# Low parts of the keys on all 128 rows: a second score product with 128 rows instead of 64

## The chip, the cores and the metric

The kernel runs on one core of one Trainium2 chip. The metric is the device time of one execution in microseconds. The kernel before has a median of 1945.59 us over 3 runs (1942.4 to 1946.55). Five engines work side by side, each on its own list of instructions, and wait for one another by semaphores: TensorE (PE, matrix products), VectorE (DVE), ScalarE (ACT), GpSimd (POOL) and SyncE (SP, which issues the transfers).

## The reference

Two layers over 512 latent tokens and 256 context tokens of width 1024: attention with a feed-forward part, then a gated linear recurrence with another. Only attention is touched:

```python
q_l = apply_axial_rope(rms_norm(q, q_norm), rope)      # 16 heads of 64
k_all = concat([rms_norm(k_ctx), apply_axial_rope(rms_norm(k_lat))])   # 4 key heads, 768 keys
s = einsum('bkgqd,bksd->bkgqs', q, k) * 64 ** -0.5     # float32
p = softmax(s); o = einsum('bkgqs,bksd->bkgqd', p, v)
y = o @ w_o
```

Four query heads share a key head. Latent queries see all 768 keys, context queries the 256 context keys.

## The kernel before, in words

The products run in a short float32 form (float32r). To keep float32 accuracy, an operand is split into a high part (rounded to the short form) and a low part (the rest), and the products high by high, high by low and low by high are added in one PSUM bank (`mm3`, L105 to L107, for the projections).

**Tiles.** Tokens come in 6 tiles of 128 (4 latent, 2 context). A head has 64 numbers per token, so after a transpose a head fills 64 rows. The 128 rows of a query tile hold both parts of the same head: the high part on one half and the low part on the other (`qd`, L545 and L546; which half is high depends on whether the key head g is even). The high keys stand twice, once on each half (`kd`, L525, written in both places before the transpose), so that one product of 128 rows gives high query by high key plus low query by high key (L606). The low keys of two key heads share one tile, one on each half (`kTl`), and the second product (L607) takes just the 64 rows with the high query: high query by low key.

**Preparation.** Queries and keys are made in `qk_norm_rope`, in units of two token tiles: 3 key units and 12 query units. A unit is squared on ACT (L479, tile `qsq`), reduced and turned into a scale on DVE and ACT (L482 to L489), scaled (L491, `qhat`), rotated on DVE and POOL (L501 to L510, tiles `qrot`, two buffers, and `qsin`), split into high and low (L525 and L526 for keys, L545 and L546 for queries), then transposed by PE into a PSUM bank and copied out by ACT (L537 for keys, L555 for queries). While a unit goes through this chain, PE makes the projections of the following ones (`q`, four PSUM banks). The transposes of a unit are issued three units later (`Q_LAG`).

**The attention loop.** 16 heads by 6 query tiles make 96 units. Each step of the loop issues the score products of unit i (two PSUM buffers `sc`; max on DVE L647, exponential on ACT L649, reciprocal on DVE L650, scaling on POOL L651), the transposes of unit i-3 (PE L661; ACT casts the high part `pth`, DVE subtracts the low part `ptl`), and every second step the product with the values of units up to i-6 (PE L672 and L673, collected in `ofp`). When two heads are complete, their outputs are split into `oh` and `ol` (three buffers each), and after four heads the output projection (`wo`) is run piece by piece between the units.

**What sets the order.** The code is written with these lags, and when the program is built a scheduler may let an instruction change places with others of its engine. The order is then fixed; each engine takes its list in that order.

Of the kernel before, what the change touches and what calls it, by code (L numbers as in the profile page):

```python
# [8 lines left out]
F32 = mybir.dt.float32  # L9
F32R = mybir.dt.float32r  # L10
# [6 lines left out]
P = 128  # L17
# [4 lines left out]
T = NL + NC  # L22
NT = T // P
NLT = NL // P
EPS = 1e-6
HEADS = 16
KVH = 4
HD = 64
# [15 lines left out]
def kernel(  # L44
# [10 lines left out]
    PE, DVE, ACT, POOL = nc.tensor, nc.vector, nc.scalar, nc.gpsimd  # L55
    dma = nc.sync.dma_start

    def pool(name, es=None, **kw):
        return (es or ctx).enter_context(tc.tile_pool(name=name, bufs=1, reuse_waits="tile", **kw))
# [76 lines left out]

    pes = psum_pool(s2=3, b=2)

# [1 line left out]
    ident = cst.tile([P, P], F32, name="ident")  # L140
    make_identity(nc, ident)
    ones = cst.tile([P, P], F32, name="ones")
# [84 lines left out]
        return ring.tile([P, 1024], F32, tag="raw", bufs=4, name=name)  # L227


# [1 line left out]
    def sumsq_add(acc, sqp, h, k, first, eng=None):  # L231
        if first:
            ACT.activation(acc, h, AF.Square)
        else:
            sq = sqp.tile([P, T], F32, tag="sq", bufs=2, name=f"sq{k}")
            sq = sq[:, : h.shape[1]]
            ACT.activation(sq, h, AF.Square)
            (eng or DVE).tensor_tensor(acc, acc, sq, op=ALU.add)
# [53 lines left out]
        lo = [pl.tile([P, T], F32R, name=f"hnl{k}") for k in range(KT)]  # L292
        return hi, lo

    # ================= layer 0: attention =================
    qes = ctx.enter_context(ExitStack())
    hnp = pool("hn0p", qes, side="right")
    hn_hi, hn_lo = hn_tiles(hnp)
    qst = pool("qkvst", qes, side="right")

# [1 line left out]
    vvs = ctx.enter_context(ExitStack())  # L302
    vvp = pool("vvp", vvs)
    vvt = vvp.tile([P, NT, KVH, P], F32R, name="vv")
# [36 lines left out]
    for t in range(NT):  # L341
        r = rs0[:, t : t + 1]
# [44 lines left out]
    for k in range(KT):  # L387
        ps = s2(f"ptx{k}")
        for t in range(NT):
            PE.transpose(ps[:, t * P : (t + 1) * P], xt[t][:, k * P : (k + 1) * P], ident)  # L390
        h = stp.tile([P, T], F32, name=f"xhT{k}")
# [3 lines left out]
            DVE.tensor_copy(h, ps[:, 0:T])  # L395
        xhT.append(h)

    kraw = qst.tile([P, NT, 256], F32, tag="kraw", name="kraw")
    accs = [s2(f"kv{i}") for i in range(3)]
    acc = [accs[t // 2][:, (t % 2) * 512 : (t % 2) * 512 + 512] for t in range(NT)]  # L400
    def kv_load(k0, n):
# [30 lines left out]
    DVE.tensor_copy(cols2[:, 16:48], pr[:, 0:32])  # L432
    st.close()

# [1 line left out]
    att = ctx.enter_context(ExitStack())  # L436
    keep = pool("attkeep", att)

    def qt_tile(g):
        return keep.tile([P, 4, T], F32R, tag=f"qT{g}", name=f"qT{g}")  # L440

    qT = [qt_tile(g) for g in range(KVH)]
    kTt = keep.tile([P, KVH + KVH // 2, T], F32R, name="kT")
    kTh = [kTt[:, g] for g in range(KVH)]
    kTl = [kTt[:, KVH + i] for i in range(KVH // 2)]

    ropec = qst.tile([P, NLT, HD], F32, name="ropec")
    ropes = qst.tile([P, NLT, HD], F32, name="ropes")
    dma(ropec, rope_cos.rearrange("(t p) d -> p t d", p=P))
    dma(ropes, rope_sin.rearrange("(t p) d -> p t d", p=P))  # L450
    tabs = {}
# [19 lines left out]
    def qk_norm_rope(src, tp, nm, eng=POOL):  # L471
        w, cw, sw = tabs[nm]

        def tmp(tag, bufs=1):
            tt = qst.tile([P, 512], F32, tag=tag, bufs=bufs, name=tag)
            return tt.rearrange("p (t h d) -> p t h d", t=2, d=HD)

        sq = tmp("qsq")
        ACT.activation(sq, src, AF.Square)  # L479
        sst = qst.tile([P, 3, 8], F32, tag="ss", bufs=2, name="ss")  # L480
        ss, sr, sa = sst[:, 0], sst[:, 1], sst[:, 2]
        DVE.tensor_reduce(ss, sq.rearrange("p t h d -> p (t h) d"), op=ALU.add, axis=AX.X)  # L482
        DVE.tensor_scalar(ss, ss, 1.0 / HD, EPS, op0=ALU.mult, op1=ALU.add)
        ACT.activation(sr, ss, AF.Sqrt)
        DVE.reciprocal(sr, sr)
        DVE.tensor_tensor(sa, sr, sr, op=ALU.mult)
        DVE.tensor_tensor(sa, sa, ss, op=ALU.mult)
        DVE.tensor_scalar(sa, sa, -0.5, 1.5, op0=ALU.mult, op1=ALU.add)
        DVE.tensor_tensor(ss, sr, sa, op=ALU.mult)  # L489
        qh = tmp("qhat")  # L490
        DVE.tensor_tensor(qh, src, ss.rearrange("p (t h) -> p t h", t=2).unsqueeze(3).to_broadcast([P, 2, 4, HD]),  # L491
                          op=ALU.mult)
        r = tmp("qrot", 2)
        if tp == 2:
            eng.tensor_tensor(r.rearrange("p t h d -> p (t h) d"), qh.rearrange("p t h d -> p (t h) d"),
                               w.unsqueeze(1).to_broadcast([P, 8, HD]), op=ALU.mult)
            return r
        sn = tmp("qsin")
        for tt in range(2):
            t = tp * 2 + tt  # L500
            DVE.tensor_tensor(r[:, tt], qh[:, tt], cw[:, t].unsqueeze(1).to_broadcast([P, 4, HD]), op=ALU.mult)  # L501
            sn5 = sn[:, tt].rearrange("p h (a b i) -> p h a b i", a=2, b=2)
            q5 = qh[:, tt].rearrange("p h (a b i) -> p h a b i", a=2, b=2)
            t5 = sw[:, t].rearrange("p (a b i) -> p a b i", a=2, b=2)
            for b in range(2):
                POOL.tensor_tensor(
                    sn5[:, :, :, b], q5[:, :, :, 1 - b],
                    t5[:, :, b].unsqueeze(1).to_broadcast([P, 4, 2, 16]), op=ALU.mult,
                )
        DVE.tensor_tensor(r, r, sn, op=ALU.add)  # L510
        return r

    for i in range(NT // 2):
        kv = accs[i].rearrange("p (t n) -> p t n", t=2)
        vsrc = kv[:, :, 256:512].rearrange("p t (g d) -> p t g d", d=HD)
        dst = vvt[:, 2 * i : 2 * i + 2]
        ACT.copy(kraw[:, 2 * i : 2 * i + 2], kv[:, :, 0:256])
        split(dst[:, :, :, 0:HD], dst[:, :, :, HD:P], vsrc)

    def k_first(tp):  # L520
        r = qk_norm_rope(kraw[:, 2 * tp : 2 * tp + 2].rearrange("p t (h d) -> p t h d", d=HD), tp, "k")
        kd = qst.tile([P, 2, KVH, 2, HD], F32R, tag="sp", bufs=3, name="kd")
        kl = qst.tile([P, 2, KVH, HD], F32R, tag="spl", name="kl")
        for i in range(2):
            DVE.tensor_copy(kd[:, :, :, i].rearrange("p t h d -> p (t h) d"), r.rearrange("p t h d -> p (t h) d"))  # L525
        POOL.tensor_tensor(kl, r, kd[:, :, :, 0].bitcast(F32), op=ALU.subtract)  # L526

        def second():
            kds = [kd[:, :, g].rearrange("p t a d -> p t (a d)") for g in range(KVH)]
            kds += [kl[:, :, 2 * i : 2 * i + 2].rearrange("p t a d -> p t (a d)") for i in range(KVH // 2)]  # L530
            for i in range(0, len(kds), 2):
                pt = bank("ptk")
                for j in range(2):
                    for tt in range(2):
                        PE.transpose(pt[:, (2 * j + tt) * P : (2 * j + tt + 1) * P],
                                     kds[i + j][:, tt].bitcast(F32), ident)
                ACT.copy(kTt[:, i : i + 2, tp * 256 : tp * 256 + 256], pt.rearrange("p (g t) -> p g t", g=2))  # L537

        return second

# [55 lines left out]

    def score_mm(h, t):
        g, j = h // 4, h % 4
        hrow = slice((g % 2) * HD, (g % 2) * HD + HD)
        keys = key_tiles(t)  # L600
        nk, k0 = len(keys) * P, keys[0] * P
        q = qT[g][:, j, t * P : (t + 1) * P]
        ps = s2("sc")
        for a in range(0, nk, 512):
            e = min(nk, a + 512)
            PE.matmul(ps[:, a:e], q, kTh[g][:, k0 + a : k0 + e], start=True, stop=False)  # L606
            PE.matmul(ps[:, a:e], q[hrow], kTl[g // 2][hrow, k0 + a : k0 + e], start=False, stop=True)  # L607
        return ps

    dfill.drain()  # L610
# [28 lines left out]
    ap_ = pool("att", att)  # L639
# [54 lines left out]
    fill.add(residual_in())  # L694
    pfill.add(ada_chunk(4, None, lambda: ap_.tile([P, T], F32, tag="pf", bufs=4, name="arows"), ring_raw))
    units = [(h, t) for h in range(HEADS) for t in range(NT)]
    pfs, pts, ofps, ohs = {}, {}, {}, {}

    def second(h, t):
        if t % 2 == 0:  # L700
# [6 lines left out]
    def third(h, t):  # L707
        if t % 2 == 0:
            return
        if h % 2 == 0 and t == 1:  # L710
            ofps[h // 2] = ap_.tile([P, T], F32, tag="sq", bufs=2, name="ofp")
        pv_prod(h, t // 2, *pts.pop((h, t // 2)), ofps[h // 2])
        if h % 2 == 1 and t == NT - 1:
            a = ap_.tile([P, T], F32R, tag="oh", bufs=3, name="oh")
            b = ap_.tile([P, T], F32R, tag="ol", bufs=3, name="ol")
            split(a, b, ofps.pop(h // 2), DVE if h == HEADS - 1 else POOL)
            ohs[h // 2] = (a, b)
            if h % 4 == 3:
                g = h // 4
                prs = [ohs.pop(2 * g), ohs.pop(2 * g + 1)]  # L720
                fill.add(wo_gen(g, [p_[0] for p_ in prs], [p_[1] for p_ in prs]))
# [15 lines left out]
    pes.close()  # L737
    pes = ctx.enter_context(psum_pool(s2=3, b=2))

    # ================= feed-forward =================  # L740
    def ffn(layer, only_lat, begin, late, pre=None, tail=None):
        n = NL if only_lat else T
        spans = SP2[:1] if only_lat else SP2
# [215 lines left out]

    ffn(0, False, lambda fill, fp: fill.add(ada_ffn(0, 5, fp)), ada_last, tail=norm_tail)  # L960

    # ================= layer 1: gated linear recurrence =================
    hg = ExitStack()
    hop = pool("hgrno")
    hp = pool("hgrn", hg)
# [312 lines left out]
```

## Time and profile before

| What | Value |
|---|---|
| Runs | 1945.59 us median, 1942.4 to 1946.55 |
| Span of the profiled execution | 1940.9 us, 4.7 us below the median; no other time is recorded for it |
| PE busy over the span | 1881.8 us, 97% |
| DVE, ACT, POOL busy | 1128.3 us (58%), 679.6 us (35%), 394.6 us (20%) |
| Score products, first and last start | 173.3 and 454.3 us |
| Preparation of queries and keys | to 173.3 us; the last 80 us of it are 95 to 175 us |
| Mean granted clock of PE | 0.992 |

Busy shares over the whole span mix stages with different limits, so the stretches are read apart. In the order of time, durations on PE overlap: a product's cost there is the distance between its start and the next start. A row of waits names the waiting engine and line, what it waited for, the total in us, how often, and the longest. "issue" means that an engine stood still without waiting for anything that the profile shows.

### The profile page before, as it was taken

What the parts mean: (1) busy time and instruction counts of PE and PEld (TensorE: products, weight loads), DVE (VectorE), ACT (ScalarE), POOL (GpSimd) and SP (SyncE); (2) the same over time, 40 slices, a digit from 0 to 9 for tenths busy, and PEclk for the clock granted to TensorE, in tenths of its full rate; (3) what the DMA queues carried; (4) which work ended last, traced back from release to release, by engine and by line L of the source; (5) the groups of instructions that cost most, each with busy time, mean ns of one, the idle gap of its engine ahead of it and who ended that gap; (6) DMA issues with size and microseconds to landing.
All of it is one profiled execution on the core that took longest, in us unless ns stands there. A gap on an engine that the chain in (4) does not pass through costs nothing. (4 is left out here: it accounts for less than half of the span.)

```text
span 1940.9 us, 29657 instructions
## 1 busy us (share of the span) xinstructions
PE 1881.8 (97%) x12111; PEld 1636.6 (84%) x12111; DVE 1128.3 (58%) x1815; ACT 679.6 (35%) x1219; POOL 394.6 (20%) x401
## 2 busy tenths in 40 slices
PE   8999999999999999999999999999999899999998
PEld 6787677777888888888887888989898799898997
DVE  4675677776993736544545546464656754344444
ACT  3334766564422112212222523333233332222224
POOL 1253434332200000000001434453446100000000
PEclk9999999999999999999999999999999999999999
DMA  9434100001442425433422111211211133333321
GB/s 327 160 99 141 55 1 23 4 20 46 128 147 60 152 60 153 138 98 118 139 68 75 51 55 38 66 55 55 65 34 44 44 99 96 90 95 90 98 81 61
DMA packets 206152, 166.37 MB, mean 86 GB/s; under 512 B 6801, under 2 KB 189249, under 8 KB 206017
## 3 DMA queue, kind: packets, MB, share of 16 engines
q1 hardware_dynamic: 205728, 163.43, 27.3%
q8 instruction: 96, 1.57, 0.3%
q10 hardware_dynamic: 288, 1.05, 0.1%
q14 instruction: 40, 0.32, 0.1%
HBM read 162.36 MB, written 2.10 MB: 85 GB/s over the span
## 5 line engine op out<-in xcount | busy, mean ns | idle before, releaser
L105 PE MATMUL ffi<-fnh,whi_fi 128*128 128x258 f32 (+2 forms) x1408 | 440.3, 313 | 1.4 <-ACT fnh L769 1.3
L106 PE MATMUL ffi<-fnl,whi_fi 128*128 128x258 f32 (+2 forms) x1408 | 439.3, 312 | 2.3 <-DVE fnl L770 2.3
L107 PE MATMUL ffi<-fnh,wlo_fi 128*128 128x258 f32 (+2 forms) x1408 | 437.5, 311 | 0.0
L106 PEld LDWEIGHTS ffi<-fnl,whi_fi 128*128 128x128 f32 x1408 | 268.1, 190 | 19.0 <-DVE fnl L770 3.4
L105 PEld LDWEIGHTS ffi<-fnh,whi_fi 128*128 128x128 f32 x1408 | 266.8, 190 | 17.9 <-ACT fnh L769 1.5
L107 PEld LDWEIGHTS ffi<-fnh,wlo_fi 128*128 128x128 f32 x1408 | 267.0, 190 | 15.8
L82 ACT CAST whi_fi<-raw_fi 128x1024 fp32r<-128x1024 f32 x88 | 92.3, 1050 | 362.9 <-issue 194.2
L250 POOL TENSOR_TENSOR rc<-rc,mhalf 128x2 f32<-128x2 f32 (+2 forms) x6 | 6.4, 1068 | 927.9 <-DVE rc L248 927.9
L105 PE MATMUL ffo<-gh,whi_fo 128*128 128x512 f32 (+1 forms) x542 | 192.2, 355 | 1.5 <-DVE hT L637 1.0
L107 PE MATMUL ffo<-gh,wlo_fo 128*128 128x512 f32 (+1 forms) x542 | 190.8, 352 | 0.0
L106 PE MATMUL ffo<-gl,whi_fo 128*128 128x512 f32 (+1 forms) x542 | 190.7, 352 | 0.0
L637 DVE SCALAR_TENSOR_TENSOR hT<-ffo,modc,hT 128x512 f32<-128x512 f32 (+1 forms) x74 | 47.9, 648 | 128.7 <-PE ffo L107 128.7
L222 DVE SCALAR_TENSOR_TENSOR adacc<-adw,csil,adacc 128x1024 f32<-128x1024 f32 x70 | 88.3, 1281 | 54.9 <-DMA adw<-in_ada_w_dram 54.7
L82 ACT CAST whi_fo<-raw_fo 128x896 fp32r<-128x896 f32 (+1 forms) x48 | 47.0, 980 | 203.6 <-PE ffo L106 106.3
L105 PEld LDWEIGHTS ffo<-gh,whi_fo 128*128 128x128 f32 x542 | 101.9, 188 | 17.4 <-issue 2.1
L106 PEld LDWEIGHTS ffo<-gl,whi_fo 128*128 128x128 f32 x542 | 101.9, 188 | 15.4
L107 PEld LDWEIGHTS ffo<-gh,wlo_fo 128*128 128x128 f32 x542 | 101.8, 188 | 15.4
L1092 POOL TENSOR_TENSOR KD<-KD,tot 128x384 f32<-128x384 f32 x96 | 100.1, 1065 | 68.8 <-ACT kc L1075 67.2
L85 DVE TENSOR_TENSOR wlo_fi<-raw_fi,whi_fi 128x1024 fp32r<-128x1024 f32 x87 | 106.2, 1222 | 8.0 <-ACT whi_fi L82 7.0
L651 POOL TENSOR_SCALAR pf<-pf,st 128x768 f32<-128x768 f32 (+1 forms) x96 | 73.3, 765 | 164.3 <-DVE st L650 146.6
L85 DVE TENSOR_TENSOR ptl<-pt,pth 128x384 fp32r<-128x384 f32 (+1 forms) x160 | 80.4, 526 | 26.6 <-ACT pth L82 24.9
L647 DVE TENSOR_REDUCE st<-sc 128x1 f32<-128x768 f32 (+1 forms) x96 | 74.4, 775 | 34.5 <-PE sc L607 34.0
(305 smaller groups left out, 4199.3 us busy)
## 6 DMA issues: line engine op xcount, KB each, us to landing
raw_fi<-in_ffn_w_in_dram SPq DMA_DIRECT2D x88, 512.0 KB, 3.7
adw<-in_ada_w_dram SPq DMA_DIRECT2D x80, 512.0 KB, 3.9
raw_fo<-in_ffn_w_out_dram SPq DMA_DIRECT2D x32, 448.0 KB, 3.6
raw_fo<-in_ffn_w_out_dram SPq DMA_DIRECT2D x16, 512.0 KB, 3.7
raw_hz<-in_hgrn_w_in_dram SPq DMA_DIRECT2D x14, 512.0 KB, 3.7
adr<-in_ada_w_dram SPq DMA_DIRECT2D x16, 256.0 KB, 5.0
adr<-in_ada_w_dram SPq DMA_DIRECT2D x8, 512.0 KB, 7.1
raw_wq<-in_attn_w_qkv_dram SPq DMA_DIRECT2D x8, 512.0 KB, 5.1
```

The lines of the kernel that those rows point to most:

```text
L82: ACT.copy(hi, src)
L85: (eng or DVE).tensor_tensor(lo, src, hi.bitcast(F32), op=ALU.subtract)
L105: PE.matmul(ps, ahi, bhi, start=first, stop=False)
L106: PE.matmul(ps, ahi, blo, start=False, stop=False)
L107: PE.matmul(ps, alo, bhi, start=False, stop=last)
L222: DVE.scalar_tensor_tensor(a, raw, cc, a, op0=ALU.mult, op1=ALU.add)
L250: POOL.tensor_tensor(rc, rc, mhalf.to_broadcast([P, nt]), op=ALU.pow)
L637: DVE.scalar_tensor_tensor(hT[o][:, a:e], ps, mcol(layer, ch, o, v), hT[o][:, a:e], op0=ALU.mult, op1=ALU.add)
L647: DVE.tensor_reduce(st3[:, 0:1], ps[:, :nk], op=ALU.max, axis=AX.X, negate=True)
L651: POOL.tensor_scalar(pf, pf, st3[:, 2:3], 1.0, op0=ALU.mult, op1=ALU.mult)
L1092: eng.tensor_tensor(view, view, f, op=ALU.mult)
```

## The change

The low keys of each key head now stand on both halves of the 128 rows, as the high keys do. The tile `kT` grows from 6 to 8 planes of 768 columns. The second score product takes the whole query tile and these low keys, so that it adds low query by low key as well. After the transposes of the low keys, ACT copies each half to the upper 64 rows and DVE to the lower 64 rows, two copies each in place of one copy of 128 rows.

Space is made elsewhere. The raw keys become three tiles of two token tiles each, one of which shares the buffer of `qsin`. The squares and the two rotation tables use the ring `qrot` of two buffers, in which the rotated result also lies. The head outputs `oh` and `ol` use one new tile for the first four heads, and then the query tiles of the key head before, which are no longer read. Some comment lines go, with no effect.

```diff
-    kraw = qst.tile([P, NT, 256], F32, tag="kraw", name="kraw")
+    kraw = [qst.tile([P, 2, 256], F32, tag="kraw" if tp else "qsin", bufs=2 if tp else 1, name="kraw")
+            for tp in range(NT // 2)]
...
-    kTt = keep.tile([P, KVH + KVH // 2, T], F32R, name="kT")
+    kTt = keep.tile([P, 2 * KVH, T], F32R, name="kT")
     kTh = [kTt[:, g] for g in range(KVH)]
-    kTl = [kTt[:, KVH + i] for i in range(KVH // 2)]
+    kTl = [kTt[:, KVH + g] for g in range(KVH)]
-    ropec = qst.tile([P, NLT, HD], F32, name="ropec")
-    ropes = qst.tile([P, NLT, HD], F32, name="ropes")
+    ropec = qst.tile([P, NLT, HD], F32, tag="qrot", bufs=2, name="ropec")
+    ropes = qst.tile([P, NLT, HD], F32, tag="qrot", bufs=2, name="ropes")
...
-        sq = tmp("qsq")
+        sq = tmp("qrot", 2)
...
-                ACT.copy(kTt[:, i : i + 2, tp * 256 : tp * 256 + 256], pt.rearrange("p (g t) -> p g t", g=2))
+                pg = pt.rearrange("p (g t) -> p g t", g=2)
+                if i < KVH:
+                    ACT.copy(kTt[:, i : i + 2, cs], pg)
+                    continue
+                for j in range(2):
+                    dst = kTt[:, KVH + j : 2 * KVH : 2, cs]
+                    rows = slice(j * HD, (j + 1) * HD)
+                    ACT.copy(dst[0:HD], pg[rows])
+                    DVE.tensor_copy(dst[HD:P], pg[rows])
...
-        hrow = slice((g % 2) * HD, (g % 2) * HD + HD)
...
-            PE.matmul(ps[:, a:e], q[hrow], kTl[g // 2][hrow, k0 + a : k0 + e], start=False, stop=True)
+            PE.matmul(ps[:, a:e], q, kTl[g][:, k0 + a : k0 + e], start=False, stop=True)
...
-            a = ap_.tile([P, T], F32R, tag="oh", bufs=3, name="oh")
-            b = ap_.tile([P, T], F32R, tag="ol", bufs=3, name="ol")
+            if h % 4 == 1:
+                o4s[0] = qt_tile(h // 4 - 1) if h >= 4 else ap_.tile([P, 4, T], F32R, name="o4")
+            i2 = h % 4 - 1
+            a, b = o4s[0][:, i2], o4s[0][:, i2 + 1]
```

PE's instructions keep their order over the whole program, and so do SP's; on POOL one subtraction of the preparation changes places. What moves is on DVE and ACT in the preparation, while the first key and query units go through. The first place is on DVE, where the second key unit is rotated and the query unit after it follows (`ss` are the small scale columns, `qhat` the scaled unit, `kd` the doubled high keys, `wlo_wq` the low part of a query weight). Before:

```order
L491 TENSOR_TENSOR qhat<-kraw,ss 128x512
L545 CAST qd<-qrot 128x8x64
L501 TENSOR_TENSOR qrot<-qhat,cwk 128x256 x2
L482 TENSOR_REDUCE ss<-qsq 128x8
L510 TENSOR_TENSOR qrot<-qrot,qsin 128x512
L483 TENSOR_SCALAR ss<-ss 128x8
L525 CAST kd<-qrot 128x8x64 x2
L485 RECIPROCAL ss<-ss 128x8
L482 TENSOR_REDUCE ss<-qsq 128x8
```

And now:

```order
L492 TENSOR_TENSOR qhat<-kraw,ss 128x512
L502 TENSOR_TENSOR qrot<-qhat,cwk 128x256 x2
L547 CAST kT<-ptk 64x2x256
L511 TENSOR_TENSOR qrot<-qrot,qsin 128x512
L483 TENSOR_REDUCE ss<-qrot 128x8
L526 CAST kd<-qrot 128x8x64 x2
L547 CAST kT<-ptk 64x2x256
L484 TENSOR_SCALAR ss<-ss 128x8
L85 TENSOR_TENSOR wlo_wq_1136<-raw_wq_1134,whi_wq_1135 128x1024
```

The cast of the query unit ahead (`qd`) no longer stands between the scaling and the rotation, and the two copies of the first key unit (L547) stand inside the second one's rotation. The second place is on ACT, at the key copies of the first unit (`ptk` is the PSUM bank of the transposes). Before:

```order
L484 ACTIVATE ss<-ss 128x8 x2
L479 ACTIVATE qsq<-q_866 128x512
L537 CAST kT<-ptk 128x2x256 x3
L479 ACTIVATE qsq<-kraw 128x512
L484 ACTIVATE ss<-ss 128x8 x2
```

And now:

```order
L485 ACTIVATE ss<-ss 128x8
L541 CAST kT<-ptk 128x2x256 x2
L546 CAST kT<-ptk 64x2x256
L480 ACTIVATE qrot<-q_868 128x512
L546 CAST kT<-ptk 64x2x256
```

The three wide copies became two wide and two of 64 rows, and the next square, now into the ring `qrot`, stands between the latter.

More of the change, by code (lines that the diff above doesn't have):

```diff
@@ L516 @@
         dst = vvt[:, 2 * i : 2 * i + 2]
-        ACT.copy(kraw[:, 2 * i : 2 * i + 2], kv[:, :, 0:256])
+        ACT.copy(kraw[i], kv[:, :, 0:256])
         split(dst[:, :, :, 0:HD], dst[:, :, :, HD:P], vsrc)
     def k_first(tp):
-        r = qk_norm_rope(kraw[:, 2 * tp : 2 * tp + 2].rearrange("p t (h d) -> p t h d", d=HD), tp, "k")
+        r = qk_norm_rope(kraw[tp].rearrange("p t (h d) -> p t h d", d=HD), tp, "k")
         kd = qst.tile([P, 2, KVH, 2, HD], F32R, tag="sp", bufs=3, name="kd")
@@ L530, in second @@
             kds += [kl[:, :, 2 * i : 2 * i + 2].rearrange("p t a d -> p t (a d)") for i in range(KVH // 2)]
+            cs = slice(tp * 256, tp * 256 + 256)
             for i in range(0, len(kds), 2):
@@ L696 @@
     units = [(h, t) for h in range(HEADS) for t in range(NT)]
-    pfs, pts, ofps, ohs = {}, {}, {}, {}
+    pfs, pts, ofps, ohs, o4s = {}, {}, {}, {}, {}
     def second(h, t):
```

## The prediction

> **What bounds the kernel now.** I first read the page for the span, then the busy times of the stretch of attention, then who waited for whom in it, and last the single instructions of the score products.
>
> ```profile
> span 1940.9 us, 29657 instructions
> 175.00:460.00 285.00, 282.70 (x1618) 210.64 (x1617) 201.61 (x447) 184.05 (x426) 106.35 (x114) 0.99 0.11 35
> PE pt L661 <- DVE ptl L85: 1.2, 2, 0.6
> PE po L672 <- ACT pth L82: 0.5, 2, 0.2
> PE sc L606 <- ACT pf L649: 0.3, 1, 0.3
> ```
>
> The second row is the stretch from 175 to 460 us, which is the attention loop: its length, then the busy time of PE, weight loads, DVE, ACT and POOL, the clock and the DMA share. PE is busy for 282.7 of 285.0 us at a clock of 0.99, and the three rows behind it are all the waits of PE in the stretch: 2.0 us. DVE works 201.6 us and ACT 184.1. So PE sets the length of attention, and what PE saves there shortens it until the next engine is full.
>
> The order of time on PE shows where PE's own time goes. The columns are start, duration, engine, line and operation; durations overlap, so the cost of a product is the distance to the next start.
>
> ```profile
> 301.08 0.40 PE L105 MATMUL wo<-oh,whi_wo 128*128 128x512 f32 x1
> ...
> 302.24 0.39 PE L107 MATMUL wo<-oh,wlo_wo 128*128 128x512 f32 x1
> 302.47 0.40 PE L606 MATMUL sc<-kT,qT 128*128 128x512 f32 x1
> 302.80 0.50 PE L607 MATMUL sc<-kT,qT 64*128 64x512 f32 x1
> 303.22 0.39 PE L606 MATMUL sc<-kT,qT 128*128 128x256 f32 x1
> 303.54 0.38 PE L607 MATMUL sc<-kT,qT 64*128 64x256 f32 x1
> 303.85 0.44 PE L661 MATMUL pt<-ident,pf 128*128 128x128 f32 x2
> ...
> 304.25 0.28 PE L106 MATMUL wo<-ol,whi_wo 128*128 128x256 f32 x1
> ...
> 304.85 0.39 PE L606 MATMUL sc<-kT,qT 128*128 128x512 f32 x1
> ```
>
> Six products of 512 columns with 128 rows run from 301.08 to 302.47: 0.232 us each. Five of 256 columns run from 304.25 to 304.85: 0.12 us each. The four score products between them, of the same widths, take 0.33, 0.42, 0.32 and 0.31 us. Both members of a pair are slow, the 128-row one too, so the price is not that of the 64-row product alone: it is paid at each change between 64 and 128 rows.
>
> ```profile
> 301.31 0.19 PEld L107 LDWEIGHTS wo<-oh,wlo_wo 128*128 128x128 f32 x1
> 302.24 0.19 PEld L606 LDWEIGHTS sc<-kT,qT 128*128 128x128 f32 x1
> 302.79 0.18 PEld L607 LDWEIGHTS sc<-kT,qT 64*128 64x128 f32 x1 [0.36 <-issue]
> ```
>
> The weight loads say the same. Between products of 128 rows the next load starts while the one before still streams (302.24, with the product of L107). The load of the 64-row product starts only at 302.79, after 0.36 us in which the loader waited for nothing that the profile shows.
>
> **The change part by part.** *The score products.* All of them now have 128 rows, in PE's old order; no matmul is added.
>
> ```profile
> L606 PE MATMUL sc<-kT,qT x160: 275/386/502, 173.3 to 454.1; 128*128 128x256 f32 x96, 128*128 128x512 f32 x64
> L607 PE MATMUL sc<-kT,qT x160: 378/383/579, 173.8 to 454.3; 64*128 64x256 f32 x96, 64*128 64x512 f32 x64
> ```
>
> There are 64 units with both widths (a latent query tile of one head) and 32 with 256 columns alone. The trace of before has no score pair of two 128-row products; the nearest rows are the L105 to L107 products above, which also load the same left operand twice in a row and add into one bank. By them a pair costs 2 x 0.232 or 2 x 0.12 us. A full unit falls from 303.85 - 302.47 = 1.38 to 0.70 us and saves 0.68; a narrow one, by 303.22 to 303.85, from 0.63 to 0.24 and saves 0.39. That is 64 x 0.68 + 32 x 0.39 = 43.5 + 12.5 = 56 us of PE time. The bounds are 0 and 56.
>
> *What of it is on the path.* 285.0 - 56 = 229 us is PE's floor. DVE comes next:
>
> ```profile
> DVE st L647 <- PE sc L607: 34.0, 44, 5.5
> DVE ptl L85 <- ACT pth L82: 24.9, 45, 1.2
> DVE st L650 <- ACT pf L649: 15.7, 19, 1.7
> DVE hT L637 <- PE wo L107: 4.2, 12, 0.6
> DVE ofp L676 <- ACT ofp L675: 1.1, 5, 0.2
> ```
>
> DVE waits 38.2 us for PE (34.0 + 4.2) and 41.7 us for ACT (24.9 + 15.7 + 1.1). A faster PE ends the first sort. The second is handed over inside a softmax unit (ACT's cast, then DVE's subtraction; ACT's exponential, then DVE's reciprocal), and nothing of it is edited. If it stays whole, DVE needs 201.6 + 41.7 = 243.3 us, more than PE's 229. Two errors lie in this, of opposite sign: some of the waits for ACT are ACT's own waits for PE passed on and will shrink, and some of the waits for PE stay, above all while the pipeline fills:
>
> ```profile
> DVE st L647 <- PE sc L607: 9.9, 5, 5.5
> ```
>
> That is the same wait in 175 to 200 us alone. I let the two cancel and take 243.3 us: attention is shorter by **41.7 us**, and 14 of PE's 56 us are handed back as waits of PE for the probabilities. Bounds: 56 (PE's floor) and 32 (41.7 less the 9.9).
>
> *The keys.* Each of three key units (two token tiles each) loses one ACT copy of 128x512 and gets two on ACT and two on DVE, each of 64x512. Three more for ACT, six for DVE.
>
> ```profile
> 95.00:110.00 15.00, 11.56 (x89) 9.70 (x88) 12.92 (x28) 5.23 (x11) 9.31 (x9) 0.89 0.23 69
> DVE kd L525 <- POOL qrot L495: 1.2, 1, 1.2
> DVE qrot L510 <- POOL qsin L506: 1.0, 2, 0.8
> L491 DVE TENSOR_TENSOR qhat<-q,ss 128x512 f32<-128x512 f32 x12 | 8.3, 692 | 0.9
> ```
>
> The first row has the columns of the stretch of attention above, the last is from the groups by line (busy time, mean ns of one, idle before). No DVE copy of this form is in the trace; L491 reads 512 columns of PSUM in 0.69 us, and I take that, with 0.43 as the lower end (the 512-column cast of L545 below, from SBUF). In the stretch where the keys are made DVE is full: 12.92 busy + 2.2 of waits for POOL = 15.1 of 15 us. Four of the six copies fall there in the new order, so the preparation grows by 4 x 0.69 = **2.8 us**; the last two fall where DVE has room. ACT is busy 5.2 of 15 us there, and its three copies cost nothing.
>
> *Sharing of buffers.* The square of a unit and its rotated result now take turns in one ring of two; before, the result had both. So a unit's first product into its result waits until POOL has subtracted from the result of the unit before.
>
> ```profile
> 155.28 0.60 ACT L479 ACTIVATE qsq<-q 128x512 f32<-128x512 f32 x1 [3.10 <-PE q L107]
> 159.44 1.03 DVE L501 TENSOR_TENSOR qrot<-qhat,cwq 128x256 f32<-128x256 f32 x2
> 162.45 0.43 DVE L545 CAST qd<-qrot 128x512 fp32r<-128x512 f32 x1
> 162.96 1.30 POOL L546 TENSOR_TENSOR qd<-qrot,qd 128x512 fp32r<-128x512 f32 x1 [1.34 <-DVE qd L545]
> 166.40 1.02 DVE L501 TENSOR_TENSOR qrot<-qhat,cwq 128x256 f32<-128x256 f32 x2
> ```
>
> A result is held from 159.44 to 162.96 + 1.30 = 164.26, 4.8 us, and the next unit wants its buffer at 166.40, 7.0 us after the first. So the wait is hidden by 2.2 us where one unit comes per 7 us. In the first group key and query units alternate, six in about 21 us (three of the 7.0), and 6 x 4.8 = 29 would not fit: up to 8 us more. I keep 0 in the sum and 8 in the range. If DVE stands there, the next query's reduction, and behind it PE's transposes, are late. The head outputs go into query tiles whose last score product is 18 units back (unit 23 against step 41 for the first), and SP's transfers keep their order: 0 for both.
>
> *Sum.* 1940.9 - 41.7 + 2.8 = 1902.0 us for the span. The profiled execution's span lies 4.7 us below the median of 1945.6; with that the median becomes **1906.7**, say 1907 us.
>
> **The rivals.**
>
> *PE stays the bound* (15%): the waits for ACT were PE's all along and vanish. PE is busy 99% now, and DVE's bare 201.6 us lie under 229; against it, 41.7 us of handovers would have to overlap fully. Attention takes 229, the total 1945.6 - 56 + 2.8 = 1892 us.
>
> *Two score buffers become the bound* (12%). A unit's product needs the buffer whose exponential, two units back, is done.
>
> ```profile
> L647 DVE TENSOR_REDUCE st<-sc 128x1 f32<-128x768 f32 x64 | 61.1, 954 | 28.8 <-PE sc L607 28.6
> L649 ACT ACTIVATE pf<-sc,st 128x768 f32<-128x768 f32 x64 | 58.0, 906 | 21.6 <-DVE st L647 19.9 <-PE pta L175 1.0 <-DVE st L650 0.4
> ```
>
> The loop is 0.70 + 0.95 + 0.91 = 2.6 us, and 243.3/96 x 2 = 5.1 us pass per two units, so it decides only if 2.5 us of queueing on DVE and ACT join it. With 3.0 us, 5.6 x 48 = 269 us: 16 gained, 1945.6 - 16 + 2.8 = 1932 us.
>
> *No gain* (4%): the second product still cannot load its weights beside the first, since both take the same rows of the array and the same left operand. Each second product would then keep its 0.42 us, the first its 0.33. Time: 1945.6 + 2.8 = 1948 us, within 0.2%. Against it stand the L105 and L107 loads above, which overlap with equal rows. The Trainium skill ("TensorE: Matmul & The Clock Gate", Part 3, "The mechanism") says just this against the change: a weight load overlaps a running product only when the row group differs. By that rule the result is this rival; the trace disagrees, with the load of L606 at 302.24 beside the product of L107, both on all 128 rows.
>
> *Slower* (4%): the ring of two makes the units of the preparation strictly serial, square to subtraction. A unit takes 155.28 to 164.26, 9.0 us, and 15 of them 135 us, against some 80 us now (95 to 175): 55 more, 1945.6 - 41.7 + 55 = 1959 us. It outweighs the gain from 80 + 41.7 = 122 us on, 8.1 us a unit. Against it: in the new order the next unit's reduction (into the other buffer) stands ahead of the present unit's cast, so only the 4.8 us are serial.
>
> **How the numbers follow.** Forecast 65%, 1907 us, own range 1894 to 1924 (1945.6 - 56 + 4, and 1945.6 - 32 + 2.8 + 8). PE's floor gives the low end, 1889 with no price for the copies. From 1889 to 1924 it holds the forecast and the first rival, 80%; the last three, 20%, are left out. What can be told from no change is about 0.2%, 4 us. Faster: 65 + 15 + 12 = 92%; the same 4%; slower 4%.
>
> **What would show it.** In the changed profile the second score product (L616 there) should be 128*128, the starts in a unit 0.23 and 0.12 us apart, and its weight load should start beside the first product, with no "issue" gap. Attention should last about 243 us, DVE's waits for scores should fall from 34 to under 10, and PE should show some 14 us of waits for pth, ptl and the exponential. First score at about 176 us instead of 173.3. The prediction is wrong if the pairs keep their 1.38 us, if PE waits over 25 us in attention, or if the preparation grows by more than 8 us.

## The result

| | before | changed |
|---|---|---|
| Median | 1946.07 us (4 runs, 1942.4 to 1952.79) | 1901.60 us (4 runs, 1899.95 to 1901.97) |
| Span of the profiled execution | 1940.9 us | 1899.4 us |
| Ratio | | 0.9766, 95% interval 0.9745 to 0.9788 |

The change saves 44.5 us of the median and 41.5 us between the two profiled spans; the profiled execution of before was one of its quicker ones (granted clock 0.992; the other executions of the kernel before on record have 0.985 to 0.992). The forecast was 1907 us.

### The profile page after: what moved, and what is told of

Same layout as the page of the kernel before. It is cut to its first block, busy times and chain, and to the rows that moved or that the text cites. A ratio compares the mean times of both kernels' runs of the same rounds, so it can differ in the third digit from the quotient of the medians.

```text
span 1899.4 us, 29674 instructions
## 1 busy us (share of the span) xinstructions
PE 1833.4 (97%) x12111; PEld 1633.3 (86%) x12111; DVE 1127.6 (59%) x1821; ACT 680.3 (36%) x1222; POOL 394.8 (21%) x401
## 5 line engine op out<-in xcount | busy, mean ns | idle before, releaser
L85 DVE TENSOR_TENSOR wlo_fi<-raw_fi,whi_fi 128x1024 fp32r<-128x1024 f32 x87 | 106.1, 1221 | 7.5 <-ACT whi_fi L82 6.5
L85 DVE TENSOR_TENSOR ptl<-pt,pth 128x384 fp32r<-128x384 f32 (+1 forms) x160 | 79.5, 522 | 9.7 <-ACT pth L82 8.4
L1103 DVE TENSOR_TENSOR QD<-QD,tot 128x256 f32<-128x256 f32 x96 | 56.3, 626 | 42.2 <-PE lv L1096 42.0
```

The source lines that it names most:

```text
L85: (eng or DVE).tensor_tensor(lo, src, hi.bitcast(F32), op=ALU.subtract)
L1103: eng.tensor_tensor(view, view, f, op=ALU.mult)
```

## The profile after

The order of time on PE and its weight loads in the changed kernel first (start, duration, engine, line, operation):

```profile
283.51 0.40 PE L615 MATMUL sc<-kT,qT 128*128 128x512 f32 x1
283.51 0.19 PEld L616 LDWEIGHTS sc<-kT,qT 128*128 128x128 f32 x1
283.75 0.39 PE L616 MATMUL sc<-kT,qT 128*128 128x512 f32 x1
283.98 0.28 PE L615 MATMUL sc<-kT,qT 128*128 128x256 f32 x1
284.09 0.28 PE L616 MATMUL sc<-kT,qT 128*128 128x256 f32 x1
284.21 0.28 PE L681 MATMUL po<-pth,vv 128*128 128x256 f32 x1
```

A full unit runs from 283.51 to 284.21: 0.70 us against 1.38. The weight load of the second product starts at 283.51, together with the first product, with no gap ahead of it. The other weight loads aren't shown.

The rows of single lines give the stage's two ends: the first score product (L606 before, in the prediction, at 173.3 us; L615 now) and the last value product. The kernel before:

```profile
L673 PE MATMUL po<-ptl,vv x224: 274/282/388, 194.0 to 462.4; 128*128 128x256 f32 x112
```

And of the changed kernel:

```profile
L615 PE MATMUL sc<-kT,qT x160: 277/283/507, 178.9 to 411.4; 128*128 128x256 f32 x96, 128*128 128x512 f32 x64
L682 PE MATMUL po<-ptl,vv x224: 274/281/385, 196.7 to 419.7; 128*128 128x256 f32 x112
```

So the account of the span is:

| | before | changed | difference |
|---|---|---|---|
| Up to the first score product | 173.3 | 178.9 | +5.6 |
| First score to last value product | 289.1 | 240.8 | -48.3 |
| From there to the end | 1478.5 | 1479.7 | +1.2 |
| Span | 1940.9 | 1899.4 | -41.5 |

Attention of the changed kernel by the view of stretches (length, then busy time and count of PE, its weight loads, DVE, ACT and POOL, granted clock, share and GB/s of DMA):

```profile
179.00:420.00 241.00, 234.42 (x1640) 206.44 (x1640) 200.67 (x453) 184.06 (x430) 107.08 (x115) 0.99 0.15 45
```

The waits of DVE in the changed kernel from 175 to 420 us (sum, count, longest):

```profile
DVE st L659 <- ACT pf L658: 14.4, 19, 1.6
DVE st L656 <- PE sc L616: 8.8, 8, 4.1
DVE ptl L85 <- ACT pth L82: 8.4, 28, 0.4
DVE hT L646 <- PE wo L107: 1.6, 8, 0.2
DVE ofp L685 <- ACT ofp L684: 1.3, 5, 0.5
```

And those of PE in the same stretch:

```profile
PE sc L615 <- DVE qhat L492: 3.4, 1, 3.4
PE pt L670 <- DVE ptl L85: 2.6, 7, 0.8
PE sc L615 <- ACT pf L658: 1.2, 3, 0.7
PE po L681 <- ACT pth L82: 0.8, 2, 0.4
```

DVE waits 10.4 us for scores and projections (38.2 before) and 24.1 us for ACT (41.7 before). PE's 3.4 us for `qhat` lie ahead of the first score product and were there before; the three other rows make 4.6 us, and two more waits, of 0.4 and 0.3 us, bring that to 5.3.

## The experiments

**The product alone.** The theory: PE pays at each change between 64 and 128 rows. The rival: the time came from the other edits.

```diff
-            PE.matmul(ps[:, a:e], q[hrow], kTl[g // 2][hrow, k0 + a : k0 + e], start=False, stop=True)
+            PE.matmul(ps[:, a:e], q, kTl[g // 2][:, k0 + a : k0 + e], start=False, stop=True)
```

> The kernel before with one edit: the second score product takes all 128 rows of the query tile and of the old shared tile of low keys, so it adds low query times the low keys of the neighbouring key head, which the reference does not have; no copy, buffer or tile is changed. Theory (the price is paid at each change between 64 and 128 rows): attention shortens as in the changed kernel, by about 48 us from its first score product to its last value product, the first score product starts at 173 us as before, and the time is about 1946 - 48 = 1898 us, under the changed kernel's 1901.6. Rival (the gain came from the moved head outputs or the new order of the preparation): about 1946 us.

Measured: 1896.3 us (1893.3 to 1896.8), ratio 0.9731 (0.9714 to 0.9748).

The rows of the first score product and of the last value product in its profile:

```profile
L605 PE MATMUL sc<-kT,qT x160: 277/282/507, 174.9 to 407.0; 128*128 128x256 f32 x96, 128*128 128x512 f32 x64
L672 PE MATMUL po<-ptl,vv x224: 274/281/386, 192.4 to 415.3; 128*128 128x256 f32 x112
```

Attention takes 415.3 - 174.9 = 240.4 us, as in the changed kernel (240.8). The product alone brings the whole gain, and without the preparation's price it is 5.3 us under the changed kernel by the medians. Only the version below that leaves out the low probabilities is faster, at 1895.5 us. The term that it adds, low query times the low keys of the neighbouring head, is a product of two low parts, as is the term that the kernel before leaves out. The end of the preparation, the first score product, moved by 1.6 us here although no edit touches the preparation: one subtraction on DVE took 2.33 us instead of 1.22, PE waited 1.9 us instead of 0.9 for a later one, and the granted clock from 125 to 140 us was 0.89 instead of 1.00. So differences under 2 us in that number aren't read below.

**The preparation alone.** The changed kernel with its product undone:

```diff
+        hrow = slice((g % 2) * HD, (g % 2) * HD + HD)
...
-            PE.matmul(ps[:, a:e], q, kTl[g][:, k0 + a : k0 + e], start=False, stop=True)
+            PE.matmul(ps[:, a:e], q[hrow], kTl[g][hrow, k0 + a : k0 + e], start=False, stop=True)
```

> The changed kernel with the second score product back on 64 rows (of the doubled low keys): all copies, buffers and orders of the change, without its product. Theory: score units take 1.38 us again, the first score product starts at 179 us instead of 173, and the time is 1946 + 5.6 + 1 = about 1952 us. Rival (the gain came from the buffers): about 1902 us.

Measured: 1949.5 us (1947.5 to 1953.7; 1952 expected), ratio 1.0016 (1.0003 to 1.0028), and the first score product at 179.0 us. The preparation costs 5.7 us up to the first score in the profiled execution, the slowest of the ten; the whole time is longer by 0.6 to 5.5 us. By the medians the two halves make -50.5 and +2.8, together -47.7 against -44.5 for both: they add up to within about 3 us.

**Both products on 64 rows.** Is a 64-row product slow by itself, or the change of rows?

```diff
-            PE.matmul(ps[:, a:e], q, kTh[g][:, k0 + a : k0 + e], start=True, stop=False)
-            PE.matmul(ps[:, a:e], q, kTl[g][:, k0 + a : k0 + e], start=False, stop=True)
+            PE.matmul(ps[:, a:e], q[hrow], kTh[g][hrow, k0 + a : k0 + e], start=True, stop=False)
+            PE.matmul(ps[:, a:e], q[hrow], kTl[g][hrow, k0 + a : k0 + e], start=False, stop=True)
```

> The changed kernel with both score products on the 64 rows of the high query; low query times high key is left out. No rows change inside a unit, only at its two ends. Theory (price at each change of rows): a full unit has two changes instead of four and falls from 1.38 to about 1.04 us, a narrow one keeps 0.63; 64 x 0.34 = 22 us less than with the product alone undone, so 1952 - 22 = about 1930 us. Rival (a product of 64 rows is slow by itself): all four products are slow, 1.38 us or more for a full unit, about 1952 us or more.

Measured: 1930.4 us (1927.4 to 1931.4), 19.2 us under the preparation alone by the medians, 22 expected. A unit in order of time, with the two products ahead of it:

```profile
300.85 0.28 PE L106 MATMUL wo<-o,whi_wo 128*128 128x256 f32 x1
300.97 0.28 PE L107 MATMUL wo<-o,wlo_wo 128*128 128x256 f32 x1
301.18 0.49 PE L616 MATMUL sc<-kT,qT 64*128 64x512 f32 x1
301.51 0.39 PE L617 MATMUL sc<-kT,qT 64*128 64x512 f32 x1
301.75 0.28 PE L616 MATMUL sc<-kT,qT 64*128 64x256 f32 x1
301.87 0.27 PE L617 MATMUL sc<-kT,qT 64*128 64x256 f32 x1
302.07 0.87 PE L671 MATMUL pt<-ident,pf 128*128 128x128 f32 x6
```

In the middle of the unit the 64-row products take 0.24 and 0.12 us, the times of 128-row products of these widths. Only the first (0.33) and the last (0.20, before the next tile of 128 rows) are longer, by 0.10 and 0.08 us. The product of 128 rows just ahead of the unit pays too: 0.21 us from 300.97, where the one before it took 0.12. The rows are free; the change is not, and both of its neighbours pay. The rival falls.

**The same products, grouped.** The kernel before with both 128-row products of a unit first:

```diff
-        for a in range(0, nk, 512):
-            e = min(nk, a + 512)
+        spans = [(a, min(nk, a + 512)) for a in range(0, nk, 512)]
+        for a, e in spans:
             PE.matmul(ps[:, a:e], q, kTh[g][:, k0 + a : k0 + e], start=True, stop=False)
+        for a, e in spans:
             PE.matmul(ps[:, a:e], q[hrow], kTl[g // 2][hrow, k0 + a : k0 + e], start=False, stop=True)
```

> The kernel before with the products of a full unit in another order: both on 128 rows first, then both on 64. The same products, the same preparation. Theory: two changes of rows instead of four in the 64 full units, 22 us of PE time, and PE stays the bound, since 285 - 22 = 263 is over DVE's 243: about 1946 - 22 = 1924 us. Rival (a product of 64 rows is slow by itself): 1946 us.

Measured: 1920.0 us (1917.3 to 1921.1), ratio 0.9855 (0.9840 to 0.9869): 26.8 us saved by the medians where 22 were expected, by an order alone.

The same two rows here:

```profile
L606 PE MATMUL sc<-kT,qT x160: 274/364/508, 173.8 to 430.9; 128*128 128x256 f32 x96, 128*128 128x512 f32 x64
L674 PE MATMUL po<-ptl,vv x224: 274/282/389, 192.9 to 439.2; 128*128 128x256 f32 x112
```

Attention falls from 289.1 to 439.2 - 173.8 = 265.4 us, so 23.7 of the 25.7 us between the two profiled spans lie there.

**What holds attention above PE's floor.** The changed kernel without DVE's subtraction for the low probabilities:

```diff
-            split(pth[:, i0 : i0 + n, qs], ptl[:, i0 : i0 + n, qs],
-                  pt[:, : n * P].rearrange("p (k q) -> p k q", q=P))
+            ACT.copy(pth[:, i0 : i0 + n, qs], pt[:, : n * P].rearrange("p (k q) -> p k q", q=P))
...
-            PE.matmul(po[:, 0:256], vv[kt][:, g, :], ptl[:, i, :], start=False, stop=(i == len(keys) - 1))
+            PE.matmul(po[:, 0:256], vv[kt][:, g, :], pth[:, i, :], start=False, stop=(i == len(keys) - 1))
```

> The changed kernel without DVE's subtraction that makes the low part of the probabilities; the second value product reads the high part instead, so the low part is left out and PE's count of products stays. DVE falls by about 80 us (128 x 0.55 + 32 x 0.42). Theory (what keeps attention at 241 us above PE's 233 is DVE's place in the handovers of a unit): the stage falls to about 233 us, the time to about 1894. Rival (the two score buffers or ACT): the stage stays at 240 or more, about 1901 us.

Measured: 1895.5 us (1892.4 to 1898.6); attention from 179.5 to 416.2 = 236.7 us.

Attention without its ends, by the view of stretches, in the changed kernel and here:

```profile
181.00:411.00 230.00, 223.78 (x1571) 197.31 (x1570) 191.49 (x433) 176.93 (x414) 102.09 (x108) 0.99 0.13 41
181.00:411.00 230.00, 223.50 (x1595) 199.57 (x1593) 130.99 (x287) 177.37 (x420) 102.82 (x109) 0.99 0.13 41
```

Its waits of PE (sum, count, longest), those that grew:

```profile
PE sc L615 <- ACT pf L658: 2.6, 9, 0.4
PE wo L106 <- POOL qT L85: 2.5, 2, 1.3
PE wo L106 <- POOL o L85: 1.2, 1, 1.2
```

With DVE's work in this window down from 191 to 131 us the stage loses 4.1 us, half of what was expected. PE's waits for the subtraction are gone, but waits for ACT's exponentials and for POOL's low part of the head outputs (3.7 us) stand in their place, and PE is idle for 6.5 of the 230 us where it was for 6.2. So the edit is worth 4.1 us, but not by less idle time of PE: where they come from isn't shown, and that DVE is what holds attention isn't either.

**The ring alone.** The kernel before with one edit of the preparation:

```diff
-        sq = tmp("qsq")
+        sq = tmp("qrot", 2)
```

> The kernel before with one edit: the square of a unit takes its buffer from the ring of the rotated results. No copies of low keys are added, the score products stay as they were. The preparation of the changed kernel is 5.6 us longer. If the ring is the cause (it holds up units and changes the order in which DVE splits the query weights), the first score product starts at about 178 us and the time is about 1951. If the six copies on DVE are the cause, it starts at 173 to 175 us and the time is 1946 to 1948.

Measured: 1950.5 us (1948.0 to 1952.4), ratio 1.0021 (1.0013 to 1.0030), first score product at 175.6 us. The two expectations named the time and the start together, and the result takes one from each: the time of "the ring is the cause", the start of "the copies are". The start is 2.3 us later than before, little more than the 1.6 us seen without an edit. Between the profiled spans the loss is 7.9 us (1948.8 against 1940.9), and the rest of it lies where nothing was edited: 2.8 us in attention (467.5 - 175.6 = 291.9 against 289.1) and 2.8 us behind it (1481.3 against 1478.5; the ten profiles of this study range from 1476.0 to 1481.3 there). In attention the clock of PE drops in this profile:

```profile
402.00:410.00 8.00, 8.00 (x30) 6.32 (x31) 4.27 (x8) 3.74 (x8) 3.21 (x3) 0.57 0.01 2
```

The column after the five busy times, 0.57, is the granted clock from 402 to 410 us; the kernel before has 1.00 in that stretch. The 0.43 that are missing over 8 us are 3.4 us at full clock, enough for the 2.8 of attention. PE is busy all the time, with score products, transposes and value products. The kernel before runs the same instructions in the same order about 2 us earlier, with the same wait of 0.25 us for `pth` shortly ahead, and keeps 1.00. The preparation alone shows a drop too (0.73 in the same stretch). Why the clock falls there stays open, and so does whether it falls in the other executions: of these one mean clock each is on record, 0.986 to 0.989 here and 0.985 to 0.992 for the kernel before.

**All copies on ACT.** The changed kernel with:

```diff
-                    DVE.tensor_copy(dst[HD:P], pg[rows])
+                    ACT.copy(dst[HD:P], pg[rows])
```

> The changed kernel with all copies of the low keys on ACT, none on DVE. If the six copies on DVE are the cause of the longer preparation, the first score product starts at 173 to 176 us and the time is 1896 to 1899. If the ring is, it starts at about 178 us and the time stays at 1901.

Measured: 1898.5 us (1896.2 to 1899.2), first score product at 176.1 us, attention 416.3 - 176.1 = 240.2 us. Taking the six copies from DVE brings 2.8 us up to the first score and 3.1 us by the medians, as the first expectation has it. PE's waits in the preparation, in the changed kernel (the wait from 125 to 180 us) and in this one:

```profile
PE q L106 <- DVE wlo_wq L85: 5.1, 1, 5.1
```

With all copies on ACT:

```profile
PE q L106 <- DVE wlo_wq L85: 3.4, 1, 3.4
PE ptk L537 <- ACT qT L565: 3.0, 1, 3.0
```

The changed kernel has three smaller waits too (1.5, 1.4 and 0.5 us), so that PE waits 8.5 us there from 85 to 185 us, without the wait for `qhat`, and 6.4 us here. The copies on DVE stood ahead of the low part of a query weight (`wlo_wq`), for which PE waits with the next projections; how much of the delay is theirs is worked out further below.

**The low parts of the query weights on POOL.** The product alone, with:

```diff
-            ws.append(load_split(src, [P, 4, 256], f"wq{g}{i}"))
+            ws.append(load_split(src, [P, 4, 256], f"wq{g}{i}", POOL if g >= 2 else None))
```

> The kernel of the product alone (128 rows with the old shared low keys), and the low parts of the query weights of the last two key heads made on POOL instead of DVE. PE's waits for those low parts, 2.4 us there, should go: about 1894 us against 1896. If POOL, which takes about 2.4 us for one against DVE's 1.2, is late instead, PE waits longer and the time is 1896 or more.

Measured: 1902.0 us (1901.1 to 1905.4), 5.7 us slower than the product alone.

The wait of PE in the preparation here:

```profile
PE q L106 <- POOL wlo_wq L85: 7.3, 2, 4.9
```

PE's wait moved from DVE to POOL and grew from 2.4 to 7.3 us. The second expectation holds.

## Why the prediction was right

**The bound and the price.** PE was the bound, and the price sat at the change of rows. The unit fell to the forecast 0.70 us, the product alone gives the whole gain, and two experiments that keep 64-row products but take out part of the changes save 19 and 27 us where 22 were forecast for each. So the 56 us of PE time were right in kind. The row of the prediction in which the 128-row product of a pair was also slow (0.33 and 0.32 us) carried this. The Trainium skill says it as a rule ("TensorEngine Tiling (Array Packing)", "Key Properties"): changing the tiling mode, not just the tile, drains the engine. The traces agree, and add the price: about 0.2 us for a change, half of it in the product ahead and half in the product behind (the unit of both on 64 rows).

In size the 56 us were too many. The prediction priced a narrow unit at 0.63 us, by the narrow pair inside a full unit. A narrow unit by itself, in the kernel before:

```profile
311.69 0.28 PE L606 MATMUL sc<-kT,qT 128*128 128x256 f32 x1
311.90 0.38 PE L607 MATMUL sc<-kT,qT 64*128 64x256 f32 x1
312.21 0.39 PE L672 MATMUL po<-pth,vv 128*128 128x256 f32 x1
```

It takes 0.52 us, because ahead of its first product there is no change of rows. For 32 narrow units that is 3.5 us less to save.

**The rival of no gain** fell as the weight loads of before had shown: equal rows don't keep a load from overlapping. The Trainium skill's rule for it ("TensorE: Matmul & The Clock Gate", "The mechanism"), that loads overlap a running product only when the row group differs, does not hold here: the load of L616 at 283.51 starts with the product of 283.51, in the same rows.

**The term that was mis-sized.** Attention lost 48.3 us, not 41.7. The step that was mis-sized is the one that let DVE's 41.7 us of waits for ACT stand whole. They fell to 24.1: above all the wait of the subtraction for the cast, from 24.9 to 8.4 us. ACT's casts had themselves been waiting for PE's transposes, and passed the delay on; the wait of the casts, before and now:

```profile
ACT pth L82 <- PE pt L661: 44.9, 48, 2.0
ACT pth L82 <- PE pt L670: 18.8, 32, 1.3
```

The prediction had named this error and set another against it, the waits for PE that stay; those came to 10.4 us, so the two did not cancel. DVE's sum became 200.7 + 24.1 + 10.4 = 235 of 241 us.

PE's idle time grew from 2.3 us (285.0 less 282.7) to 6.6 us (241.0 less 234.4). So PE handed back 4.3 us, not 14.3, and its own time fell by about 48.3 + 4.3 = 52.6 us, which is the 56 less the 3.5 of the narrow units. PE is still the fullest engine; that DVE would set the length is the part of the mechanism that did not come. With the measured 52.6 and 5.6 (the preparation, below) the path of the forecast would give 1945.6 - 52.6 + 14.3 + 5.6 = 1913 us, and that of the first rival, PE as the bound, 1899 us. The measured 1901.6 lies nearer the rival.

**The rivals of the bound.** PE's floor of 229 us was not reached: the stretch of 285.0 us became 236.7 long, and with the narrow units at their own price the floor is 232.5. Nor did the two score buffers decide: PE waits 1.2 us for them (L615 for the exponential). The preparation grew by 5.6 us and not by the 55 of strictly serial units.

**The preparation** cost 5.6 us, not 2.8, inside the 0 to 8 that was added for the ring. The wait did not lie where the prediction looked for it, at a unit's buffer. The changed DVE list in order of time (L547 are the last two copies of low keys):

```profile
124.01 0.69 DVE L511 TENSOR_TENSOR qrot<-qrot,qsin 128x512 f32<-128x512 f32 x1 [0.78 <-POOL qsin L507]
...
126.76 0.68 DVE L547 CAST kT<-ptk 64x512 fp32r<-64x512 f32 x1
...
128.32 0.69 DVE L547 CAST kT<-ptk 64x512 fp32r<-64x512 f32 x1
...
132.24 0.69 DVE L511 TENSOR_TENSOR qrot<-qrot,qsin 128x512 f32<-128x512 f32 x1 [1.18 <-POOL qsin L507]
132.97 0.43 DVE L555 CAST qd<-qrot 128x512 fp32r<-128x512 f32 x1
133.31 1.22 DVE L85 TENSOR_TENSOR wlo_wq<-raw_wq,whi_wq 128x1024 fp32r<-128x1024 f32 x1
```

The low part of a weight stands behind the two copies and behind a rotation that waits for POOL, and PE stands still until 134.59:

```profile
134.59 0.58 PE L106 MATMUL q<-wlo_wq,hnh 128*128 128x256 f32 x1 [5.11 <-DVE wlo_wq L85]
```

The same subtraction (L85) in the kernel before and with the ring alone, and the first and the last of the rows above with all copies on ACT:

```profile
128.58 1.22 DVE L85 TENSOR_TENSOR wlo_wq<-raw_wq,whi_wq 128x1024 fp32r<-128x1024 f32 x1
130.46 1.22 DVE L85 TENSOR_TENSOR wlo_wq<-raw_wq,whi_wq 128x1024 fp32r<-128x1024 f32 x1
122.91 0.69 DVE L511 TENSOR_TENSOR qrot<-qrot,qsin 128x512 f32<-128x512 f32 x1 [0.77 <-POOL qsin L507]
130.95 1.22 DVE L85 TENSOR_TENSOR wlo_wq<-raw_wq,whi_wq 128x1024 fp32r<-128x1024 f32 x1
```

It starts 4.7 us later than before. All but DVE's copies make 2.4 us of that (130.95), the ring alone 1.9; the product alone, with the preparation of before, starts it at 129.85, 1.3 us late, so the ring's share is hardly told from chance. The copies on DVE make the other 2.4 us. That they brought 2.8 us up to the first score, the very term of the sum, is luck: the four copies that the term counts put DVE's list back by 1.1 us (124.01 against 122.91), and the last two, which the prediction put where DVE has room, by 1.3 us more.

The view of stretches around the wait, before and now:

```profile
126.00:140.00 14.00, 13.06 (x112) 12.86 (x111) 10.45 (x24) 4.68 (x10) 6.91 (x9) 1.00 0.25 76
126.00:140.00 14.00, 8.89 (x59) 8.69 (x59) 10.70 (x24) 4.46 (x8) 6.19 (x7) 0.76 0.24 75
```

Behind the wait the granted clock drops, to 0.76 over the stretch against 1.00. Other runs agree: by PE's wait and the clock from 125 to 140 us, the kernel before has 0.9 us and 1.00; the product alone 1.9 us, all copies on ACT 3.4 and the ring alone 3.6, each with 0.89; the low parts on POOL 4.9 and the preparation alone 5.1, both with 0.77. So a longer wait goes with a lower clock behind it and is paid for in part a second time; no run tests the clock by itself.

**The sum.** Forecast for the span: 1902.0; measured 1899.4. The errors are of opposite sign, and that the sum came this close is in part luck: attention was 6.6 us shorter than forecast (PE handed back 10.0 us less than forecast, and saved 3.4 us less), the preparation 2.8 us longer, and what lies behind attention 1.2 us longer, which leaves -2.6. The 4.7 us added for the median were too many: the changed kernel's median lies 2.2 us above its profiled span, and its profiled execution took 1901.45 us, 2.05 more than its span; the rest of the 4.7 was that of before being a quick one. That is the other half of the distance from 1907 to 1901.6.

## What to carry to other kernels

Read the cost of a product from start to start, and compare it with its neighbours of the same width: where both members of an alternating pair are slow, the alternation is the cost. Group products by their row count, or bring all to one count, even if the added rows hold something that is nearly nothing; the cheapest form here changed one line and copied nothing. And where the engine behind the bound waits for a third one, ask what that one waits for, before its wait is kept in the sum. Price each kind of unit by its own rows: the narrow pair inside a full unit was dearer than a narrow unit by itself.

## What was not expected

Half of the price of a change falls on the product ahead of it. In the pairs of before the first product has a change only behind it and loses 0.10 us; each of the others stands between two changes and loses 0.19, 0.20 and 0.19 us, by their distances to the next start less 0.232 or 0.12. That the two experiments saved 19 and 27 us where 22 were forecast for each fits the count of changes. In the order of PE in the traces there are 320 changes between 64 and 128 rows in attention before, 232 with both products on 64 rows (in some full units transposes stand between the score products), 194 in the grouped order and none in the changed kernel. Attention is shorter by 19.9 us (269.2, from 179.4 to 448.6) and 23.7 us in the first two, and PE's own time by 52.6 us in the last: 0.23, 0.19 and 0.16 us for each change that is gone.

The clock of PE dropped to 0.57 in the ring alone and to 0.73 in the preparation alone in a stretch of attention in which PE was busy for 8.00 and 7.70 of 8.00 us. In that stretch it did not in the kernel before, in the changed one, or with both products on 64 rows. What decides it was not tried.
